# Block 2 of a two-block transformer kernel: modulation products queued behind the first norm, and attention heads taken in pairs on halves of the systolic array

## The chip, the cores and the metric

One core of one Trainium2 chip runs one program. The metric is the device time of one execution in microseconds, the median of the runs taken. The core has engines with a queue of instructions each: TensorE (PE; its weight loads are shown as PEld), VectorE (DVE), ScalarE (ACT), GpSimd (POOL) and SyncE (SP), which issues most transfers. Each engine runs its queue in the order that was fixed when the program was built; across engines they wait for each other by semaphores. Matrix products write into eight PSUM banks, which the kernel calls `g`, `u`, `l` (two each), `t` and `f`.

## The reference

256 tokens of width 1024 in float32 go through a first block (linear attention, block attention and a product-key mixture of experts) and then through a second block of two layers. The change lies in the second. Its first layer mixes with attention, its second with a convolution, and each has an MLP with a squared ReLU behind its mixer:

```python
mod = (c_act @ ada_w[l] + ada_b[l])[:, None, :]
sh1, sc1, g1, sh2, sc2, g2 = jnp.split(mod, N_MOD, axis=-1)
h = modulate(x, sh1, sc1)
...
x = layer_norm(DEEPNORM_ALPHA * x + g1 * y, ln_g[l, 0], ln_b[l, 0])
h = modulate(x, sh2, sc2)
x = layer_norm(DEEPNORM_ALPHA * x + g2 * sq_relu_mlp(h, mlp_w1[l], mlp_w2[l]), ln_g[l, 1], ln_b[l, 1])
```

The attention of the first layer has two groups. Group a is a differential attention of 4 heads: each head has two query and key halves of 64, two softmaxes over 512 keys (256 of a context, 256 of the tokens), and the second softmax times a factor is taken from the first ahead of the values, of width 128. Group b has 8 query heads of 64 that share 2 key and value heads. The outputs of both, side by side, go through `attn_w_out`. The modulation vectors `mod` are a product of one row, the activated conditioning vector, with a matrix of 1024 x 6144 for each layer.

## The kernel before

Products that need float32 accuracy are made of three products of halves: a value is cast to a shorter float `h` (ACT, L161, or DVE), the remainder `l = raw - h` is a difference on DVE (L165) or POOL (L167), and TensorE adds `h*h`, `l*h` and `h*l` (L219 to L221 with the tokens as columns, L251 with the tokens as rows). Weights stream from HBM into `raw` tiles, by SP's queue, and get these two parts.

A scheduler sets the order of each engine's queue when the program is built, from the order in which the code is written and from simulated times. Three things override it: `issue_after(x)` puts an instruction behind `x` in the order, `in_turn()` keeps a series of products in the order in which it is written, and `behind_all` adds a real wait.

The modulation is not done on TensorE: `ada_stream` brings the matrix of both layers in 96 pieces of 128 x 1024 (`araw`, 512 KB each), and `products` multiplies each by the row `crow` and sums it into a column of `modT` (L281, one DVE operation), to which a bias is added (L282). The stream is spread over the whole program: `more(n)` emits the next n pieces, and 16 of them fall in the first MLP of block 2, whose code follows the first norm.

Group a's softmaxes come first (`a_probs`, a call for each half of 128 queries). For each of its 4 heads it calls `probs` (L1224 to L1229) for rows 0 to 63 and then for rows 64 to 127 of the query and key tiles: three products of 64 rows by 512 columns into one `u` bank (L1228), then `softmax_parts`: a maximum (L497), its negation (L499), an exponential with a sum (L503), a reciprocal (L505). Their difference is transposed by TensorE (L1234) and copied out (L1220 on ACT, L1222 on DVE, in turn). Between these lie dense products (L251) of the projections. `a_rows` makes the values (L1254).

Group b's loop follows (L1321 to L1344): for each half of the queries, four pairs of neighbouring heads 2hp and 2hp + 1, which share one key and value head and so lie on the same 64 rows. Each head gets `probs`, a scaling (L1336), four transposes (L1234) and four value products (L1340), which write the half `i` of 64 partitions of one bank `po`. A trace has two rows for each float32 product of this kind. The first products of `awo`, the output projection, for group a's half of the rows (`mx1`) lie between the pairs; the pieces 2 and 3 of `awo` for group b's half (`mx2`) come behind.

The first norm is `ln_block` at L1363. For each half `tt` of the tokens it multiplies the projection by its gate (L1124), adds the residual (L1125), takes the statistics (L1130, L1132), the inverse root (L1099 to L1103) and scales (L1147). `normed_fm` then transposes (L1025), evicts with the modulation's scale and shift into `x0`, on DVE (L1029) for `tt = 0` and on ACT (L1031) for part of it, and makes the first products of the MLP with the first weight piece in full float32 (L1034). `normed_parts` splits `x0` into `b8h` and `b8l` (L1045, L1046) behind the last scaling; its last instruction is what `behind_fm[1]` names, and it releases POOL's two products and two sums for the residual (L1155, L1156). `ln_block` is called four times; the second and third (the MLP's norm of layer one and the conv's of layer two) follow the same path.

## Time and profile before

| what | us |
|---|---|
| median of 3 runs | 1659.31 |
| lowest and highest | 1656.79, 1660.22 |
| the profiled execution | 1664.88 |
| its span | 1663.1 |
| mean granted clock of TensorE | 0.991 |

The profiled execution is one of its own, 5.6 us above the median; the trace's times start at its span's start. Block 2's group a softmaxes lie at about 1043 to 1092, group b's loop at 1104 to 1167, the first norm at 1155 to 1190, the second at 1357 to 1380, the third at 1457 to 1480. A row of the timeline gives start, duration, engine, line, operation, output and inputs, and how many like it follow; products are pipelined, so the length of a group is read from its first start to the next group's start.

### The profile page before, as it was taken

Reading aid. Unit: us, or ns where it says so; the run is one execution under the profiler, and the core shown is the slowest. Engines: PE = TensorE matmul, PEld = TensorE weight load, DVE = VectorE, ACT = ScalarE, POOL = GpSimd, SP = SyncE. Lnnn points to the kernel's source line nnn. Section 1 sums busy time; section 2 is a strip of 40 time slices with the busy share of each in tenths; the row PEclk is TensorE's granted clock in tenths of the full one; section 3 lists DMA queues with packets and bytes.
Section 4 is the critical chain, followed back from the end, with each engine's and each line's share of the span. In section 5 each row is a group of like instructions: output and inputs, shape, how many; then the busy total and the mean of one; then the engine's idle time right before and its main releaser. Section 6 shows DMA issues by size and latency. Waiting matters only on the chain.

```text
span 1663.1 us, 27669 instructions
## 1 busy us (share of the span) xinstructions
PE 1590.0 (96%) x10543; PEld 1405.8 (85%) x10543; DVE 1301.2 (78%) x2587; ACT 832.3 (50%) x1346; POOL 309.0 (19%) x219
## 2 busy tenths in 40 slices
PE   8999999999999999999999989999799999989997
PEld 5878989999999897777777778777789989989996
DVE  5777999999999988989888765686896457575445
ACT  5644433677766654444444453554454435444442
POOL 3302000233333320000000023210511124051112
PEclk9999999999999999999999999999999999999999
DMA  7424435555554468888899872031686536445540
GB/s 292 156 73 153 140 117 183 185 171 171 159 163 150 152 208 287 305 305 318 294 337 324 277 267 76 17 137 76 227 315 217 187 117 240 166 169 211 181 175 26
DMA packets 70840, 321.17 MB, mean 193 GB/s; under 512 B 7841, under 2 KB 8114, under 8 KB 54962
## 3 DMA queue, kind: packets, MB, share of 16 engines
q1 hardware_dynamic: 67808, 309.61, 54.5%
q10 hardware_dynamic: 2898, 9.78, 1.7%
q8 instruction: 83, 1.36, 0.3%
q14 instruction: 51, 0.42, 0.1%
HBM read 318.31 MB, written 1.05 MB: 192 GB/s over the span
## 4 chain that ended last, share of the span: by engine, by line
PE 51%; DVE 22%; DMA 15%; issue 7%; ACT 4%; POOL 1%; SPq 0%; DVEq 0%; ACTq 0%; POOLq 0%
PE g L251 12%; DMA araw<-in_ada_dram 7%; PE u L251 6%; DVE lu L165 5%; DMA raw<-in_vt_dram 5%; PE l L220 3%; PE l L219 3%; PE l L221 3%; PE l L864 3%; PE l L862 3%; PE l L863 3%; DVE araw L281 2%; DVE obx L896 2%; DMA raw<-in_ut_dram 2%; PE g L220 1%
## 5 line engine op out<-in xcount | busy, mean ns | idle before, releaser
L161 ACT CAST hu<-raw 128x1024 fp32r<-128x1024 f32 x244 | 256.2, 1050 | 283.3 <-DMA raw<-in_vt_dram 141.7
L165 DVE TENSOR_TENSOR l<-raw,h 128x1024 fp32r<-128x1024 f32 (+1 forms) x216 | 277.9, 1320 | 128.8 <-ACT h L161 128.8
L161 ACT CAST h<-raw 128x1024 fp32r<-128x1024 f32 x226 | 225.5, 1051 | 223.8 <-PE l L220 62.8
L165 DVE TENSOR_TENSOR lu<-raw,hu 128x1024 fp32r<-128x1024 f32 (+1 forms) x244 | 274.3, 1128 | 45.8 <-ACT hu L161 42.5
L862 PE MATMUL l<-xh,hu 128*128 128x256 f32 x928 | 261.6, 282 | 3.5 <-ACT act L872 2.6
L864 PE MATMUL l<-xh,lu 128*128 128x256 f32 x928 | 259.6, 281 | 4.0 <-DVE lu L165 3.9
L863 PE MATMUL l<-xl,hu 128*128 128x256 f32 x928 | 258.6, 279 | 0.0
L864 PEld LDWEIGHTS l<-xh,lu 128*128 128x128 f32 x928 | 174.5, 189 | 6.2 <-DVE lu L165 6.0
L862 PEld LDWEIGHTS l<-xh,hu 128*128 128x128 f32 x928 | 175.2, 189 | 4.6 <-ACT act L872 3.2
L863 PEld LDWEIGHTS l<-xl,hu 128*128 128x128 f32 x928 | 175.4, 189 | 0.1
L167 POOL TENSOR_TENSOR lu<-raw,hu 128x256 fp32r<-128x256 f32 x92 | 106.6, 1160 | 341.2 <-ACT hu L161 292.6
L167 POOL TENSOR_TENSOR l<-raw,h 128x512 fp32r<-128x512 f32 (+1 forms) x32 | 61.2, 1936 | 571.9 <-ACT h L161 510.0
L281 DVE SCALAR_TENSOR_TENSOR araw<-araw,crow 128x1024 f32<-128x1024 f32 x96 | 121.8, 1270 | 25.5 <-DMA araw<-in_ada_dram 25.2
L219 PE MATMUL l<-b8h,h 128*128 128x256 f32 x480 | 134.8, 281 | 1.2 <-ACT rl L1367 1.2
L220 PE MATMUL l<-b8l,h 128*128 128x256 f32 x480 | 134.8, 281 | 0.0
L221 PE MATMUL l<-b8h,l 128*128 128x256 f32 x480 | 134.5, 280 | 0.0
L896 DVE SCALAR_TENSOR_TENSOR obx<-cst,slotT,gpair 128x256 f16<-128x256 f32 x256 | 131.6, 540 | 1.6 <-PE u L903 1.5
L1369 POOL TENSOR_TENSOR rq<-rl 128x512 f32<-128x512 f32 x32 | 54.4, 1702 | 236.1 <-ACT rl L1367 227.8
L957 PE MATMUL g<-lu,hw 128*128 128x512 f32 x256 | 83.2, 406 | 14.8 <-DVE lu L165 14.4
L219 PEld LDWEIGHTS l<-b8h,h 128*128 128x128 f32 x480 | 90.9, 190 | 1.5 <-ACT rl L1367 1.4
L221 PEld LDWEIGHTS l<-b8h,l 128*128 128x128 f32 x480 | 90.9, 190 | 0.0
L220 PEld LDWEIGHTS l<-b8l,h 128*128 128x128 f32 x480 | 90.2, 188 | 0.1
(555 smaller groups left out, 3707.7 us busy)
## 6 DMA issues: line engine op xcount, KB each, us to landing
raw<-in_ut_dram SPq DMA_DIRECT2D x128, 512.0 KB, 4.0
raw<-in_vt_dram SPq DMA_DIRECT2D x128, 512.0 KB, 5.3
raw<-in_mw_dram SPq DMA_DIRECT2D x64, 1024.0 KB, 5.0
araw<-in_ada_dram SPq DMA_DIRECT2D x80, 512.0 KB, 5.3
raw<-in_cwi_dram SPq DMA_DIRECT2D x12, 1024.0 KB, 5.0
raw<-in_w_ina_dram SPq DMA_DIRECT2D x8, 1024.0 KB, 8.0
raw<-in_wq_dram SPq DMA_DIRECT2D x8, 1024.0 KB, 4.8
raw<-in_awi_dram SPq DMA_DIRECT2D x8, 1024.0 KB, 7.2
```

Source lines behind the costliest of these rows:

```text
L161: S.copy(h[:, c:c + w], src[:, c:c + w])
L165: V.tensor_sub(l[:, c:m], src[:, c:m], h[:, c:m].bitcast(F32))
L167: G.tensor_sub(l[:, m:c + w], src[:, m:c + w], h[:, m:c + w].bitcast(F32))
L219: PE.matmul(o, hw, xh[:, k, :], start=k == 0, stop=False)
L220: PE.matmul(o, hw, xl[:, k, :], start=False, stop=False)
L221: PE.matmul(o, lw, xh[:, k, :], start=False, stop=k == KD - 1)
L251: PE.matmul(o[:, :cw], st, mv[:, c:c + cw], start=first and kk == 0 and i == 0, stop=last and kk == kp - 1 and i == 2)
L281: V.scalar_tensor_tensor(raw, raw, 1.0, crow, ALU.mult, ALU.mult, accum_out=d)
L862: PE.matmul(o, hv[:, k], xh[:, k], start=k == 0, stop=False)
L863: PE.matmul(o, hv[:, k], xl[:, k], start=False, stop=False)
L864: PE.matmul(o, lv[:, k], xh[:, k], start=False, stop=k == KD - 1)
L896: V.scalar_tensor_tensor(ob, C("iota")[:, None, :].to_broadcast([P, 2, P]), slotT[:, 0, t:t + 1], gpair[:, t, :, None].to_broadcast([P, 2, ...
```

## The change

It has four parts.

1. `behind_fm` is made ahead of the stream of modulation pieces, and each product L281 that is emitted once it is set is ordered behind `behind_fm[1]`, the last `b8l` of the norm. It is empty until the first norm, so the first products concerned are the 16 of the first MLP.
2. `to_fm` may scale: the queries of both groups are stored times -0.125. `probs` then takes a minimum of the negated scores as the exponential's bias and -1 as its scale. The 32 negations (L499) of these heads are gone.
3. `probs` makes the scores of both row halves, six products that alternate between rows 64 to 127 and 0 to 63, in written order, into two `u` banks. Group a uses it for the two halves of a head. Group b's loop pairs heads h and h + 4, which use different key heads and so different row halves; the 16 rows of their value products alternate between the column halves 64 to 127 and 0 to 63. `PB`, the table of banks, goes.
4. As the heads' outputs now stand in pairs h, h + 4, the rows of `awo` in pieces 2 and 3 are brought in that order: each `raw` tile by two transfers of 64 partitions, both tiles issued ahead of the product.

```diff
-    behind = []
+    behind, behind_fm = [], []
...
-            V.scalar_tensor_tensor(raw, raw, 1.0, crow, ALU.mult, ALU.mult, accum_out=d)
+            with tc.issue_after(behind_fm[1]) if behind_fm else ExitStack():
+                V.scalar_tensor_tensor(raw, raw, 1.0, crow, ALU.mult, ALU.mult, accum_out=d)
...
+                if scale:
+                    S.activation(dh, pv, AF.Identity, scale=scale)
+                    V.scalar_tensor_tensor(dst[1][:, b0:b0 + nb, c0:c0 + T], pv, scale, dh.bitcast(F32), ALU.mult,
+                                           ALU.subtract)
+                    continue
...
-    def probs(qT_, kT_, qb, kb, hs, qt, tag="u"):
-        ps = bank(tag)
+    def probs(qT_, kT_, qb, kb, qt):
+        pss = [bank("u"), bank("u")]
         q_ = slice(qt * P, (qt + 1) * P)
+        next_to = in_turn()
         for n, (i, j) in enumerate(((0, 0), (0, 1), (1, 0))):
-            PE.matmul(ps, qT_[i][hs, qb, q_], kT_[j][hs, kb], start=n == 0, stop=n == 2)
-        return softmax_parts(ps, 512, sm, 512)
+            for g in (1, 0):
+                hs = slice(g * 64, g * 64 + 64)
+                next_to(pss[g], qT_[i][hs, qb, q_], kT_[j][hs, kb], start=n == 0, stop=n == 2)
+        er = []
+        for ps in pss:
+            nm = sm.tile([P, 1], F32, tag="snm", name="snm")
+            V.tensor_reduce(nm, ps, AX.X, ALU.min)
+            e = sm.tile([P, 512], F32, tag="se", name="se", bufs=4)
+            s = sm.tile([P, 1], F32, tag="ssum", name="ssum")
+            S.activation(e, ps, AF.Exp, scale=-1.0, bias=nm, accum_out=s)
+            r = sm.tile([P, 1], F32, tag="srec", name="srec")
+            V.reciprocal(r, s)
...
-            e0, r0 = probs(aqT, akT, h, h, slice(0, 64), qt, PB[qt][2 * h])
-            e1, r1 = probs(aqT, akT, h, h, slice(64, 128), qt, PB[qt][2 * h + 1])
+            (e0, r0), (e1, r1) = probs(aqT, akT, h, h, qt)
...
-            for i in range(2):
-                h = 2 * hp + i
-                g = h // 4
-                e, r = probs(bqT, bkT, h % 4, 0, slice(g * 64, g * 64 + 64), qt)
+            pts = []
+            for e, r in probs(bqT, bkT, hb, 0, qt):
                 V.tensor_scalar(e, e, r, None, ALU.mult)
-                pt = transposed(e)
-                for kt in range(4):
-                    PE.matmul(po[i * 64:i * 64 + 64, :P], bv[:, kt, g * 64:g * 64 + 64], pt[:, kt * P:(kt + 1) * P],
-                              start=kt == 0, stop=kt == 3)
+                pts.append(transposed(e))
+            next_to = in_turn()
+            for kt in range(4):
+                for g in (1, 0):
+                    next_to(po[g * 64:g * 64 + 64, :P], bv[:, kt, g * 64:g * 64 + 64], pts[g][:, kt * P:(kt + 1) * P],
+                            start=kt == 0, stop=kt == 3)
...
-    gemm_tm(wp, hp2, rows_of("awo", 2, 4), 1024, *mx2, oacc, begun=True)
+    raws = []
+    for q in range(2):
+        raws.append(wp.tile([P, 2048], F32, tag="raw", name="raw"))
+        rv = raws[q].rearrange("p (k n) -> p k n", k=2)
+        for g in range(2):
+            queued(rv[g * 64:g * 64 + 64], a["awo"][2 + g].rearrange("(i p) (k n) -> k p i n", i=2, k=2)[q])
+    gemm_tm(wp, hp2, raws, 1024, *mx2, oacc, raw=True, begun=True)
```

In the changed kernel the products made through `in_turn()` are recorded under the helper's line, L182; L251 is L250 there, L1228's scores and L1340's values are both L182, L1234 is L1255.

TensorE's queue in group b's loop, first half of the queries. Before, the six scores of a pair (`u<-bkT..`), eight rows of transposes (`l<-cst,se`), then eight value products:

```order
L1228 MATMUL u<-bkTh,bqx 128x512
L1228 MATMUL u<-bkTl,bqx 128x512
L1228 MATMUL u<-bkTh,bqx 128x512 x2
L1228 MATMUL u<-bkTl,bqx 128x512
L1228 MATMUL u<-bkTh,bqx 128x512
L1234 MATMUL l<-cst,se 128x128 x8
L1340 MATMUL f<-pt,bv 64x128 x8
L1228 MATMUL u<-bkTh,bqx 128x512
L1228 MATMUL u<-bkTl,bqx 128x512
L1228 MATMUL u<-bkTh,bqx 128x512 x2
L1228 MATMUL u<-bkTl,bqx 128x512
L1228 MATMUL u<-bkTh,bqx 128x512
```

And in the changed kernel, about the same place:

```order
L182 MATMUL u<-bkTh,bqx 128x512 x2
L182 MATMUL u<-bkTl,bqx 128x512 x2
L182 MATMUL u<-bkTh,bqx 128x512 x2
L1255 MATMUL l<-cst,se 128x128 x8
L182 MATMUL u<-bkTh,bqx 128x512
L182 MATMUL t<-pt,bv 64x128 x8
L182 MATMUL u<-bkTh,bqx 128x512
L182 MATMUL u<-bkTl,bqx 128x512 x2
L182 MATMUL u<-bkTh,bqx 128x512 x2
L1255 MATMUL l<-cst,se 128x128 x8
```

The partners of a pair stand next to each other now; the next pair's first score product has moved ahead of this pair's values, away from its five others.

DVE's queue at the first norm, where `b8h` and `b8l` are the split parts of its output, `araw` the modulation pieces and `l<-raw,h` the MLP's weight differences. Before:

```order
L281 SCALAR_TENSOR_TENSOR araw,modT<-araw,crow 128x1024
L1102 TENSOR_SCALAR qt<-qy,qh 128x1
L282 TENSOR_TENSOR modT<-modT,col 128x1
L1103 TENSOR_SCALAR qy<-qt,qy 128x1
L1147 TENSOR_SCALAR xn<-xn,mv,qy 128x512 x2
L1045 CAST b8h<-x_12732 128x4x128 x2
L1046 TENSOR_TENSOR b8l<-x_12732,b8h 128x4x128 x2
L1045 CAST b8h<-x_12732 128x2x128
L281 SCALAR_TENSOR_TENSOR araw,modT<-araw,crow 128x1024
L1045 CAST b8h<-x_12732 128x2x128
L1046 TENSOR_TENSOR b8l<-x_12732,b8h 128x2x128
L1045 CAST b8h<-x_12732 128x2x128 x2
```

In the changed kernel nothing stands between the scaling and the casts, and the casts and differences stand alone up to these rows, from the last two of each on:

```order
L1050 CAST b8h<-x_12670 128x2x128
L1051 TENSOR_TENSOR b8l<-x_12670,b8h 128x2x128
L1050 CAST b8h<-x_12670 128x2x128
L1051 TENSOR_TENSOR b8l<-x_12670,b8h 128x2x128
L281 SCALAR_TENSOR_TENSOR araw,modT<-araw,crow 128x1024 x2
L164 TENSOR_TENSOR l<-raw,h 128x1024 x2
L282 TENSOR_TENSOR modT<-modT,col 128x1
L164 TENSOR_TENSOR l<-raw,h 128x1024
L282 TENSOR_TENSOR modT<-modT,col 128x1
L164 TENSOR_TENSOR l<-raw,h 128x1024
L281 SCALAR_TENSOR_TENSOR araw,modT<-araw,crow 128x1024
```

All modulation products of this stretch have moved behind the last `b8l`, two of them ahead of the first weight differences.

ACT's queue at the second norm, with the evictions of its output (`x`, L1031, in the changed kernel L1036) and the casts of the next weights (`h<-raw`). Before:

```order
L1099 ACTIVATE qs<-mv,epst 128x1
L1031 ACTIVATE x_14431<-l,mods 128x128 x3
L1031 ACTIVATE x_14431<-t,mods 128x128 x2
L1031 ACTIVATE x_14431<-l,mods 128x128
L1031 ACTIVATE x_14431<-f,mods 128x128 x2
L161 CAST h<-raw 128x1024 x4
L1031 ACTIVATE x_14431<-l,mods 128x128 x4
```

And in the changed kernel:

```order
L1104 ACTIVATE qs<-mv,epst 128x1
L1036 ACTIVATE x_14369<-l,mods 128x128 x7
L1036 ACTIVATE x_14369<-t,mods 128x128 x2
L1036 ACTIVATE x_14369<-f,mods 128x128 x2
L160 CAST h<-raw 128x1024 x4
```

The four casts have moved behind the last evictions. The third norm has the same rows, before and after, with another number behind `x`.

## Rows read from the trace of the kernel before

**Rows 1.** The page's first part: busy time of each engine, its share of the span, and instructions.

```profile
PE 1590.0 (96%) x10543; PEld 1405.8 (85%) x10543; DVE 1301.2 (78%) x2587; ACT 832.3 (50%) x1346; POOL 309.0 (19%) x219
```

**Rows 2.** Busy time by stretch: start and end, length, then PE, PEld, DVE, ACT and POOL with their instructions, the mean granted clock of TensorE, the DMA share and GB/s. Group a's softmaxes, group b's loop, the first norm and what follows it.

```profile
1043.00:1090.00 47.00, 46.68 (x273) 36.97 (x272) 33.63 (x103) 26.49 (x58) 6.56 (x5) 1.00 0.23 90
1104.00:1167.00 63.00, 59.45 (x341) 44.85 (x340) 43.85 (x116) 27.39 (x63) 2.42 (x2) 0.97 0.23 84
1167.20:1209.00 41.80, 31.43 (x249) 30.32 (x247) 38.29 (x56) 19.58 (x31) 22.02 (x8) 0.92 0.68 239
```

**Rows 3.** PE's timeline in group a's part, one group of three score products and what follows it: start, duration, engine, line, operation, output and inputs, rows, columns.

```profile
1070.64 0.50 PE L1228 MATMUL u<-akTh,aqTh 64*128 64x512 f32 x1
...
1071.53 0.39 PE L251 MATMUL g<-h,cxl 128*128 128x256 f32 x1
```

**Rows 4.** PE's timeline in group b's loop, one cycle of a pair.

```profile
1127.28 0.49 PE L1228 MATMUL u<-bkTh,bqx 64*128 64x512 f32 x1
...
1128.87 1.10 PE L1234 MATMUL l<-cst,se 128*128 128x128 f32 x8
1130.21 1.58 PE L1340 MATMUL f<-pt,bv 128*64 128x128 f32 x16 [0.24 <-ACT pt L1220]
1131.72 0.50 PE L1228 MATMUL u<-bkTh,bqx 64*128 64x512 f32 x1
```

**Rows 5.** The same timeline in the second half of the queries, the value products of one head and what follows.

```profile
1143.52 1.09 PE L1340 MATMUL l<-pt,bv 128*64 128x128 f32 x8
1144.54 0.66 PE L1234 MATMUL l<-cst,se 128*128 128x128 f32 x4
```

**Rows 6.** PE's timeline in block 1, products through `in_turn()` (L183) on the two row halves, then on the two column halves, then on quarters.

```profile
97.34 0.71 PE L183 MATMUL u<-mkT,mqT 64*128 64x128 f32 x6
97.98 0.71 PE L523 MATMUL u<-cst,cst 128*128 128x128 f32 x4
...
112.86 0.66 PE L183 MATMUL l<-gv,at 128*64 128x128 f32 x8
113.45 0.45 PE L183 MATMUL l<-st,eb 64*64 64x128 f32 x8
```

**Rows 7.** The views of lines L1228 and L1340, what PE sat idle for ahead of them (us, times), and of L499, whose row gives least, median and most ns.

```profile
  ACT se L503: 8.2, 5
...
  ACT pt L1220: 4.2, 9
...
L499 DVE TENSOR_SCALAR snm<-sm x48: 134/144/155, 78.7 to 1150.2; 128x1 f32<-128x1 f32 x48
```

**Rows 8.** DVE's and ACT's timelines in group b's loop: both reductions of a pair, a copy of the transposes, an exponential and its read-out.

```profile
1119.35 1.28 DVE L497 TENSOR_REDUCE sm<-u 128x1 f32<-128x512 f32 x2
1120.55 0.68 DVE L1222 COPY pt<-l 128x512 f32<-128x512 f32 x1
...
1121.44 0.69 ACT L503 ACTIVATE se<-u,snm 128x512 f32<-128x512 f32 x1
1122.03 0.20 ACT L503 ACTIVATION_READ_ACCUMULATOR se<-u,snm 128x1 f32 x1
```

**Rows 9.** The chain of waits from the end of group b's loop through the first norm, in order of time: start, us, what.

```profile
1167.19 3.90 DMA araw<-in_ada_dram
1171.11 3.01 DVE araw L281 x2
1174.14 5.30 DMA araw<-in_ada_dram
1179.47 1.23 DVE araw L281 x2
...
1184.26 1.14 DVE araw L281 x2
...
1187.81 0.75 DVE b8l L1046 x2
1188.56 3.53 DVE l L165 x2
```

**Rows 10.** The timelines of DVE and POOL behind the first norm.

```profile
1196.37 2.06 DVE L281 SCALAR_TENSOR_TENSOR araw<-araw,crow 128x1024 f32<-128x1024 f32 x1
...
1198.36 3.40 DVE L165 TENSOR_TENSOR l<-raw,h 128x1024 fp32r<-128x1024 f32 x1
1201.69 3.41 DVE L281 SCALAR_TENSOR_TENSOR araw<-araw,crow 128x1024 f32<-128x1024 f32 x1
...
1188.64 6.66 POOL L1155 TENSOR_TENSOR xres<-xn,lrow 128x1024 f32<-128x1024 f32 x2 [15.62 <-DVE b8l L1046]
```

**Rows 11.** The chain of waits at the second norm and at the third.

```profile
1371.86 3.77 ACT h L161 x4
...
1376.04 4.22 PE g L1034 x32
...
1468.72 1.51 ACT x L1031 x4
1470.23 3.77 ACT h L161 x4
...
1474.41 5.78 PE g L1034 x32
```

More of the change, by code (lines that the diff above doesn't have):

```diff
@@ L35 @@
 NWARM = 9
-PB = "uuuuuuuu", "uuuuuuuu"
 EVV = 1, 0
@@ L427, in norm_rope, with to_fm @@
         return s4
-    def to_fm(src, nh, dst, c0=0, tag="u"):
+    def to_fm(src, nh, dst, c0=0, tag="u", scale=None):
         s3 = src.rearrange("p t h d -> p t (h d)")
@@ L1014, in pair @@
         return [xp2.tile([P, KD, T], F32R, tag="b8", name=n, bufs=2) for n in ("b8h", "b8l")]
-    behind_fm, hp3 = [], []
+    hp3 = []
     def normed_fm(src, tt, scale, shift, x0, w0, o0):
@@ L1212 @@
     aq = norm_rope(prj, 8, rcv, rsv, sw2, 16, V, pj, "ak", norm=False)
-    to_fm(aq, 8, aqT, 0, AQT)
+    to_fm(aq, 8, aqT, 0, AQT, -0.125)
     mx1 = [at.tile([P, 4, T], F32R, name="mx1" + c) for c in "hl"]
@@ L1314 @@
     bqT = bqx[:, 0], bqx[:, 1]
-    to_fm(bq, 8, bqT, 0, BQT)
+    to_fm(bq, 8, bqT, 0, BQT, -0.125)
     a_rows(1, pts)
@@ L1322 @@
     for qt in range(NT):
-        for hp in range(4):
-            j = qt * 4 + hp
+        for hb in range(4):
+            j = qt * 4 + hb
             for pc, tt, ns in MXO.get(j, ()):
```

7 lines of the change are left out of this document (5 added, 2 removed).

## The prediction

> **What bounds the kernel now.** The page first: PE is busy 96% of the span, DVE 78% [rows 1]. The span is mostly TensorE work, and a change gains in two ways only: fewer TensorE microseconds, or smaller holes between them. Then the table by stretches, for the places that the diff touches [rows 2]. In block 2's attention PE is nearly full: 46.68 of 47.0 us in group a's part, 59.45 of 63.0 us in group b's. At the first norm it is not: 31.43 of 41.8 us, 10.4 us of holes, with a granted clock of 0.92 on average. PE's timelines show what attention's work is made of [rows 3 to 6], the chain of waits shows what the norms' holes wait for [rows 9, 11]. The issue orders come last, for what moves without being named in the diff.
>
> **Part 1: score and value products in pairs.** A head's scores are three products of 64 rows by 512 columns. One group alone takes 0.89 us, 1070.64 to 1071.53 [rows 3]; two in sequence, on one row half and then on the same or the other, 1.59 us, 1127.28 to 1128.87 [rows 4]. Inside, a product follows the last after 0.23 us; the rest, some 0.2 us, is the step into 64-row work and out. Do products on different halves of the array run side by side? No row shows it for 512 columns on two row halves, so I bound it by block 1. There eight products on alternating column halves take 0.59 us, 112.86 to 113.45 [rows 6], 0.074 each, against 0.094 each for the sixteen value products of today (1.51 us, 1130.21 to 1131.72 [rows 4]). Eight on row and column quarters last 0.45 us as a group where those on column halves last 0.66. But six on the two row halves take 0.64 us, 97.34 to 97.98 [rows 6], 0.107 each: no gain by the mean. So the bounds for a pair of score groups are 0.99 us (three steps of 0.23, and in and out) and 1.59 us (no overlap). I take 0.99 to 1.05 where the six stand together, nearest to the column row, since the alternation is fixed in the order. The value products of a pair, 16 in eight steps: 0.97 us (8 x 0.109 and the step in), against 1.51 in the first half of the queries and 2 x 1.02 in the second, where each head's eight stand alone [rows 5].
>
> In group a's part the order cuts most pairs: one score product, some dense ones of 256 columns, then the other five. A cut pair steps in and out twice, about 1.4 us, against two neighbouring groups of 0.89 (1.69 with a shared step). In the second four pairs today's groups are cut themselves (0.99 each), and of the new pairs two are whole and two cut (1.2 on average). PE work: 4 x (1.69 - 1.41) + 4 x (1.98 - 1.2) = 4.2 us. PE is full there, so nearly all of it reaches the end; but the last two pairs stand back to back and meet the softmax. I take **3.0 us** (bounds 0 and 4.5).
>
> *A rule against this.* The step in and out is some 0.2 us [rows 3, 4]. The Trainium skill, "TensorEngine Tiling (Array Packing)", Tiling Modes, Key Properties, says that changing the tiling mode drains TensorE. The trace agrees as far as the step goes; by that rule a splintered order gives the overlap back, and were all sixteen pairs cut as the first are, the sum would be about 3 us smaller.
>
> In group b's part eight pairs save 8 x (1.59 - 0.99) = 4.8 us on scores, less five cuts at 0.2 = 3.8, and 4 x 0.54 + 4 x 1.07 = 6.4 us on values: 10.2 us of PE work. What is late next is the softmax: two reductions (1.28 us together), two exponentials of 0.69 with a read-out of 0.20 each, a scaling, a copy of 0.68 [rows 8]. With two score banks, the next pair's first product waits for this pair's last exponential: scores 0.9, reductions 1.3, the last exponential 0.9 and hand-overs, 3.3 to 3.8 us per pair. The cycle now is 4.44 us (1127.28 to 1131.72 [rows 4]). So pairs without dense products between them gain 0.7 to 1.1 us, those with dense products of `awo` beside them 1.2 to 1.6, their full saving less some wait. Waits for these results are small today: 8.2 us over both parts for exponentials, 4.2 for copies [rows 7]. I take **7.5 us** (bounds 3 and 11).
>
> The minimum in place of a negated maximum drops 32 operations of 0.144 us [rows 7], 4.6 us of DVE, 0.29 per pair; it lies in the loop just bounded and is counted there. `to_fm` has as many operations as before. The `awo` pieces come as four transfers of 512 KB for two of 1 MB, on the same queue at the same place, behind the same transfers and far ahead of their first reader. Zero for both, give or take 0.5 us; were that cover gone, one transfer's time would show.
>
> **Part 2: modulation products behind the first norm.** Attention's last product ends at 1167.2. Then the chain [rows 9] is not the norm's own: DVE takes an `ada` product of 3.01 us at 1171.11, waits 5.30 us for the next transfer to 1179.47, takes that product (1.23), and has two more (1.14, and one like it) among the casts. The last `b8l` ends at 1188.56. Foreign pieces: 3.01 + 5.30 + 1.23 + 2 x 1.14 = 11.8 us; less about 1.0 of the norm's statistics and square root that run inside them: 10.8 us gained, the last `b8l` at 1177.8. PE's 10.4 us of holes agree [rows 2].
>
> Paid back: the products still have to run. Two of them stand ahead of the first weight difference (L165), more between the next ones, and all of DVE's queue waits behind each. The same `b8l` releases POOL's products for `xres`, 6.66 us for two [rows 10], and beside POOL, DVE's operations with two inputs in SBUF take 2.06 to 3.41 us in place of 1.2. So two products cost 2.4 to 6.8 us before L165; TensorE has the second half's first products and the pieces whose differences are ready to cover some of it. I take 2.8 back, net **8.0 us** (bounds 0 and 10.8).
>
> *A rule against this too.* Beside POOL's 3.3 us operations DVE's take up to 3.41 us, alone 1.23 [rows 9, 10]. The Trainium skill, "SBUF — State Buffer", says that DVE and GpSimd take a shared port pair by an exclusive lock held for a whole instruction. The trace agrees. If every product behind the norm paid it, the net would be about 4 us in place of 8; this is rival 2.
>
> **Part 3: norms two and three, a side effect.** The order shows that these move too. Before, ACT does most of the second half's evictions (L1031), then four weight casts (L161, 3.77 us), then the last evictions; the first weight products (L1034) wait for those: casts at 1371.86, then 1376.04 for PE, and casts at 1470.23 in the third norm [rows 11]. After, all eight evictions come first, and the casts behind. The chain loses 3.77 us twice. Late next: the casts start some 1.5 us later (four evictions of 0.38 us each go first) and have the 32 products L1034 (4.22 and 5.78 us) as cover for the main product; L165 stands behind all casts of `x`, and meets POOL. I take 3.3 and 4.2 us (the 5.78 may become 4.2), less 1.5 for L165: **6.0 us** (bounds -1 and 8).
>
> **Sum.** 3.0 + 7.5 + 8.0 + 6.0 = 24.5 us. Profiled execution 1664.9 - 24.5 = 1640.4 us; it lay 5.6 us above the median of the runs, 1659.3, so against that 1634.8: **1635 us**.
>
> **Rivals.**
> 1. *Row halves don't overlap.* For: the 64-row products at 97.34. Against: those on quarters [rows 6]. Then scores gain nothing: a 0, b about 4 from values; 18 us in all, 1641.
> 2. *Products crowd DVE behind the first norm.* Five of them at up to 3.4 us meet POOL, and PE waits for L165: of the norm's 8 us 0 to 2 are left. For: [rows 10]. Against: PE's holes come before L165 today, not behind it. 17.5 us, 1642.
> 3. *Norms two and three give nothing*, since casts and L165 are late instead: 18.5 us, 1641.
> 4. *Slower.* A pair holds both score banks. If PE then went through each pair in sequence (0.9 + 1.3 + 1.8 + 0.5 + 0.55 + 0.7 + 1.0 = 6.7 us for 4.44), sixteen pairs would lose 36 us where the norms gain 14: 1681 at worst; a milder form, or the clock's 1.2 GHz level through the holes, 1663 to 1670. It decides from about 5.4 us per pair (14 / 16 above today's). Against: the next pair's scores are ordered ahead of this one's transposes and values.
> 5. *The change doesn't do what it says:* the order cuts every pair. 3 us less, 1638; in the range anyway.
>
> **How the numbers follow.** Forecast with rival 5 0.67; rivals 1, 2 and 3 0.09, 0.11 and 0.07, all still faster; rival 4 0.04; two of rivals 1 to 3 with small attention gains, no change, 0.02. Half the width of the four pairs of bounds is 2.3, 4, 5.4 and 4.5 us, 8.4 as independent terms; with 2 us between runs about 9. The range 1623 to 1649 holds that and each of rivals 1 to 3 alone. About 0.2%, 3.3 us, is what a measurement of this kernel tells from no change: faster by more 0.94, within 0.02, slower 0.04.
>
> **What would show it.** Right: a pair's six score products in about 1 us and its values in 0.97; group b's part some 55 us long for 63; at the first norm no `ada` product between attention's end and the last `b8l`, and that 11 us nearer; norms two and three without L161 in the chain between evictions. Rival 2: L281 rows above 3 us behind the norm, and holes of PE there. Wrong: holes of PE of more than 15 us in attention, or the main product behind the first norm less than 5 us nearer to attention's end.

## The result, and the profile after

The changed kernel takes 1645.08 us, the median of 4 runs (1641.12 to 1645.86), against 1659.76 us before: 14.7 us less. The ratio is 0.9896, 95% interval 0.9863 to 0.9929. In a second series of runs it is 1645.79 against 1661.46 us, 0.9892 (0.9867 to 0.9918); between them the two intervals allow a gain of 12 to 23 us. Its first profiled execution took 1644.43 us, span 1642.6 us.

What a reader compares is not the two spans but stages that begin and end with the same instruction. I take six starts on TensorE and the end: group a's first score product, the ninth product of `awo` with group a's rows (which ends group a's part), the first transposes of the first norm, the first product on the first MLP's `mh`, the first on the convolution's `cvh`, and the first on the second MLP's `mh`. Lengths between them, in us:

| profile | first score at | group a | group b | first norm | first MLP, second norm, conv | its output, third norm | second MLP to the end | from the first score |
|---|---|---|---|---|---|---|---|---|
| before | 1043.1 | 61.0 | 61.0 | 42.2 | 232.7 | 56.4 | 166.7 | 620.0 |
| before, second profile | 1043.0 | 60.9 | 61.2 | 41.9 | 236.3 | 56.1 | 166.7 | 623.2 |
| changed | 1041.5 | 62.9 | 55.5 | 33.6 | 229.7 | 51.3 | 168.1 | 601.0 |
| changed, second profile | 1045.8 | 63.0 | 55.5 | 33.5 | 231.6 | 51.8 | 167.5 | 602.9 |

From group a's first score on, the changed kernel is 17 to 22 us shorter, and most stages repeat within 0.5 us. Two things scatter more. Ahead of the first score, where the change does nothing, its start moves by 4 us between the two profiles of the changed kernel; and the stage with the first MLP moves by 3.6 us between those of before. Group a got longer by 1.9 us; group b, the norms and what follows them got shorter. The bounds don't part equal work everywhere: of the 48 products of `awo` with group b's rows, group b's stage holds 42 before and 46 after. At one each 0.23 us, 0.9 us of work moved from the first norm's stage into group b's.

The page's first part of the changed kernel, which answers to [rows 1]: the change took 12 us of TensorE's work, and DVE was busy 11 us longer. The page's groups say where: the 216 weight differences `l<-raw,h` take 289.6 us for 277.9, the modulation products hardly less than before (120.1 for 121.8).

```profile
PE 1578.2 (96%) x10543; PEld 1396.3 (85%) x10543; DVE 1312.4 (80%) x2555; ACT 833.5 (51%) x1346; POOL 302.9 (18%) x219
```

The table by stretches of both kernels, with the stages' own ends as bounds, so other rows than [rows 2]; columns as there. Before:

```profile
1043.10:1104.10 61.00, 59.25 (x356) 48.38 (x356) 47.05 (x148) 37.70 (x78) 11.04 (x7) 0.97 0.18 71
1104.10:1165.10 61.00, 57.45 (x330) 43.17 (x328) 42.74 (x113) 26.57 (x60) 2.32 (x2) 0.97 0.23 86
1165.10:1207.20 42.10, 32.34 (x255) 31.44 (x255) 37.70 (x55) 19.00 (x32) 22.02 (x8) 0.92 0.66 230
```

After:

```profile
1041.50:1104.40 62.90, 59.17 (x349) 47.73 (x348) 46.80 (x132) 37.60 (x77) 12.29 (x9) 0.95 0.21 69
1104.40:1159.90 55.50, 49.98 (x342) 35.68 (x341) 41.90 (x98) 27.14 (x62) 1.12 (x1) 1.00 0.29 94
1159.90:1193.40 33.50, 29.02 (x243) 27.88 (x242) 32.16 (x43) 19.27 (x32) 22.09 (x8) 1.00 0.62 220
```

In group a PE is busy as long as before, and idle 2 us longer. In group b it has 7.5 us less to do and is idle 5.5 us, not 3.6. At the first norm its holes shrink from 9.8 to 4.5 us. The granted clock moved too: from 0.97 to 0.95 in group a, from 0.97 to 1.00 in group b and from 0.92 to 1.00 at the first norm, so a part of the busy times is the clock's.

TensorE's timeline in group b after, one cycle and a half; it answers to [rows 4]:

```profile
1117.56 0.50 PE L182 MATMUL u<-bkTh,bqx 64*128 64x512 f32 x1
1117.56 0.73 PE L182 MATMUL u<-bkTl,bqx 64*128 64x512 f32 x2
1117.90 0.63 PE L182 MATMUL u<-bkTh,bqx 64*128 64x512 f32 x2
1118.46 0.65 PE L1255 MATMUL l<-cst,se 128*128 128x128 f32 x4
...
1124.11 0.50 PE L182 MATMUL u<-bkTh,bqx 64*128 64x512 f32 x1 [0.97 <-ACT se L1245]
1124.54 1.09 PE L182 MATMUL t<-pt,bv 128*64 128x128 f32 x16
1125.57 0.50 PE L182 MATMUL u<-bkTh,bqx 64*128 64x512 f32 x1
```

The partners start together (1117.56 twice): 512 columns on two row halves do overlap. Sixteen value products take 1.03 us, 1124.54 to 1125.57, for 1.51. But the next pair's first score product waits 0.97 us for an exponential (1124.11), in a place where TensorE waited 0.24 us for a copy before.

Around the first norm, DVE's timeline after, which answers to [rows 9, 10]:

```profile
1172.38 0.43 DVE L1051 TENSOR_TENSOR b8l<-x,b8h 128x256 fp32r<-128x256 f32 x1
1172.72 1.22 DVE L281 SCALAR_TENSOR_TENSOR araw<-araw,crow 128x1024 f32<-128x1024 f32 x1
...
1173.87 3.40 DVE L281 SCALAR_TENSOR_TENSOR araw<-araw,crow 128x1024 f32<-128x1024 f32 x1
...
1177.20 6.74 DVE L164 TENSOR_TENSOR l<-raw,h 128x1024 fp32r<-128x1024 f32 x2
```

and PE's and POOL's, the two holes that are left and what runs beside the differences:

```profile
1180.67 0.39 PE L220 MATMUL l<-b8h,l 128*128 128x256 f32 x1 [1.22 <-DVE l L164]
1183.99 0.39 PE L220 MATMUL l<-b8h,l 128*128 128x256 f32 x1 [1.67 <-DVE l L164]
...
1172.89 6.65 POOL L1160 TENSOR_TENSOR xres<-xn,lrow 128x1024 f32<-128x1024 f32 x2 [6.06 <-DVE b8l L1051]
```

The last `b8l` ends 12.9 us after the norm's first transposes (1159.9 to 1172.8), where it took 23.5 (1165.1 to 1188.6). Then the first weight differences take 3.4 us each beside POOL, and TensorE waits 2.9 us for them.

The chain of waits at the third norm after, which answers to [rows 11]:

```profile
1450.23 3.17 PE g L1039 x26
...
1454.69 1.86 ACT x L1036 x5
1456.56 3.30 ACT h L160 x4
```

The evictions end ahead of the casts, as the order said.

### The profile page after: what moved, and what is told of

Its sections match the earlier page's. It is cut to its first block, busy times and chain, and to the rows that moved or that the text cites. A ratio compares the mean times of both kernels' runs of the same rounds, so it can differ in the third digit from the quotient of the medians.

```text
span 1642.6 us, 27643 instructions
## 1 busy us (share of the span) xinstructions
PE 1578.2 (96%) x10543; PEld 1396.3 (85%) x10543; DVE 1312.4 (80%) x2555; ACT 833.5 (51%) x1346; POOL 302.9 (18%) x219
## 4 chain that ended last, share of the span: by engine, by line
PE 58%; DVE 17%; DMA 13%; issue 7%; ACT 4%; POOL 1%; SPq 0%; DVEq 0%; ACTq 0%; POOLq 0%
PE g L250 12%; PE u L250 7%; DMA raw<-in_vt_dram 5%; DMA araw<-in_ada_dram 5%; PE l L869 4%; PE l L867 4%; PE l L868 4%; DVE lu L164 4%; PE l L218 3%; PE l L219 3%; PE l L220 3%; DVE l L164 2%; DVE obx L901 2%; DMA raw<-in_ut_dram 2%; DVE araw L281 2%
## 5 line engine op out<-in xcount | busy, mean ns | idle before, releaser
L164 DVE TENSOR_TENSOR l<-raw,h 128x1024 fp32r<-128x1024 f32 (+1 forms) x216 | 289.6, 1374 | 114.7 <-ACT h L160 114.6
L160 ACT CAST h<-raw 128x1024 fp32r<-128x1024 f32 x226 | 226.3, 1053 | 227.3 <-PE l L219 56.1
L166 POOL TENSOR_TENSOR l<-raw,h 128x512 fp32r<-128x512 f32 (+1 forms) x32 | 61.2, 1936 | 561.4 <-ACT h L160 504.8
L281 DVE SCALAR_TENSOR_TENSOR araw<-araw,crow 128x1024 f32<-128x1024 f32 x96 | 120.1, 1253 | 22.4 <-DMA araw<-in_ada_dram 22.4
```

The lines of the kernel that those rows point to most:

```text
L160: S.copy(h[:, c:c + w], src[:, c:c + w])
L164: V.tensor_sub(l[:, c:m], src[:, c:m], h[:, c:m].bitcast(F32))
L166: G.tensor_sub(l[:, m:c + w], src[:, m:c + w], h[:, m:c + w].bitcast(F32))
L281: V.scalar_tensor_tensor(raw, raw, 1.0, crow, ALU.mult, ALU.mult, accum_out=d)
```

## The experiments

Twelve runs followed, each with its own profile: ten new kernels, and the two from above once more. Medians, ratios to the kernel before (same chip, same series; worked out from all runs, so not the quotient of the medians) with 95% intervals, and the stages as above:

| run | median us | ratio | group a | group b | first norm | MLP, 2nd norm, conv | 3rd norm | 2nd MLP |
|---|---|---|---|---|---|---|---|---|
| after_again (changed) | 1645.79 | 0.9892 (0.9867-0.9918) | 63.0 | 55.5 | 33.5 | 231.6 | 51.8 | 167.5 |
| e1_behind_only | 1648.96 | 0.9922 (0.9902-0.9942) | 60.8 | 62.5 | 34.4 | 229.6 | 51.3 | 168.2 |
| e2_pairs_only | 1653.30 | 0.9944 (0.9922-0.9967) | 63.1 | 56.5 | 39.7 | 232.8 | 51.9 | 167.6 |
| e3_a_alone | 1651.16 | 0.9936 (0.9913-0.9960) | 68.4 | 59.5 | 35.5 | 229.4 | 51.3 | 168.1 |
| e4_xres_late | 1637.01 | 0.9841 (0.9810-0.9872) | 62.8 | 55.2 | 30.1 | 228.8 | 51.3 | 166.6 |
| e5_a_by_head | 1647.28 | 0.9899 (0.9873-0.9926) | 67.7 | 53.3 | 33.5 | 229.5 | 51.3 | 168.1 |
| e6_b_scores_apart | 1638.84 | 0.9867 (0.9843-0.9890) | 62.8 | 52.6 | 33.6 | 229.7 | 51.3 | 168.1 |
| e7_both | 1643.46 | 0.9874 (0.9845-0.9903) | 68.8 | 54.8 | 29.7 | 229.3 | 51.3 | 166.6 |
| e8_evict_in_turn | 1659.49 | 0.9980 (0.9966-0.9994) | 62.2 | 60.9 | 41.9 | 232.5 | 51.3 | 168.2 |
| e9_a_before | 1641.90 | 0.9880 (0.9857-0.9902) | 60.9 | 56.3 | 33.9 | 229.4 | 51.9 | 167.5 |
| e10_a_before_late | 1640.20 | 0.9852 (0.9827-0.9877) | 62.1 | 56.3 | 31.7 | 229.3 | 51.3 | 166.6 |

The twelfth, before_again, was a single execution of 1668.0 us (before in that series: 1663.56). The profiled execution of a kernel often lies above its median (1650.5 for 1645.8, 1655.4 for 1649.0), so stages are compared with stages and medians with medians.

**The kernels as they are.**

> The changed kernel once more, for a tighter interval and a second profile. My reading of the two profiles is 20.4 us between them, while the medians differ by 14.7 us: I expect 13 to 18 us below the kernel before (ratio 0.989 to 0.992), since the first profile of before lay some 5 us above that kernel's own median. Rival: the first four runs happened to lie high, then about 20 us (0.988).

> The kernel before once more, profiled, to see where two profiles of one kernel differ. Theory: the scatter of some 5 us lies in block 1 ahead of group a's scores, and from there on the stages repeat within 1 us. Rival: the norm's waits for modulation transfers vary by several us, so that the first profile's 10 us hole was not typical.

The first theory held, with 15.7 us between the medians. The second held in part. Five of the six stages of before repeat within 0.3 us, the first norm's among them (41.9 us), so its holes were typical and the rival is out. But group a's first score starts at the same time in both, and the 3.6 us between them lie in the stage with the first MLP: 1.5 in the MLP itself and 1.7 in the convolution, the same 1.7 us that set the changed kernel's 231.6 apart from 229.7. Set against the medians, the 20 us between the first two profiles were partly chance.

**The two parts alone.** e1 adds part 1 of the change, the modulation products ordered behind the norm, to the kernel before:

```diff
-            V.scalar_tensor_tensor(raw, raw, 1.0, crow, ALU.mult, ALU.mult, accum_out=d)
+            with tc.issue_after(behind_fm[1]) if behind_fm else ExitStack():
+                V.scalar_tensor_tensor(raw, raw, 1.0, crow, ALU.mult, ALU.mult, accum_out=d)
```

> The kernel before with part 1 alone: modulation products ordered behind the norm's last b8l. The order shows the second and third norms' evictions ahead of the weight casts here as well. Theory (stages add): attention as before; first norm 7 us shorter, second and third 3 to 3.6 us each: about 13 us less than before, 1646 to 1649. Rival (attention's pairs were needed to get the modulation transfers out of the way, so part 1 alone is worth little): less than 6 us.

e2 takes it away from the changed kernel:

```diff
-            with tc.issue_after(behind_fm[1]) if behind_fm else ExitStack():
-                V.scalar_tensor_tensor(raw, raw, 1.0, crow, ALU.mult, ALU.mult, accum_out=d)
+            V.scalar_tensor_tensor(raw, raw, 1.0, crow, ALU.mult, ALU.mult, accum_out=d)
```

> The changed kernel without the ordering of the modulation products: pairs, scale, awo rows alone. The order of the second and third norms is the changed one here too. Theory: attention 6 us shorter, first norm as before (products among its casts), norms two and three 6 us shorter together: 10 to 13 us less than before, 1647 to 1650. Rival (norms two and three gain from the products' order): 6 us less, 1654.

e1: 12.5 us below before, about the theory's 13. The first norm is 7.8 us shorter without any pair, so the rival is out. (Group b took 1.5 us longer there: its waits are those of before, but its products take 58.9 us for 57.5, at a granted clock of 0.95 for 0.97.) e2: 8.2 us below, less than the theory's 10 to 13. Group b is 4.5 us shorter; the first norm keeps 39.7 us, and the first MLP has a hole of 2.78 us where TensorE waits 0.62 us in the kernel before, 0.87 in e1 and 1.00 in the changed kernel:

```profile
1207.67 1.22 PE L250 MATMUL g<-h,ml 128*128 128x512 f32 x2 [2.78 <-DVE ml L1399]
```

So part 1 is worth some 9 us beside the pairs, 6 at the norm and 3 by keeping this hole shut. Against the kernel before it gains nothing in the MLP itself (155.8 us in e1 from its first product to its last, 155.6 before); e1's 3.1 us in that stage are the second norm's. The third norm's 4 to 5 us come with either part.

**Norms two and three.** e8 is the kernel before with the second half's evictions in written order:

```diff
-        g = FMG[tt]
+        g, ev_ = FMG[tt], []
...
-                    a_ = S.activation(o, p_, AF.Identity, scale=scale[:, c], bias=shift[:, c])
+                    with tc.issue_after(ev_[0]) if tt and ev_ else ExitStack():
+                        a_ = S.activation(o, p_, AF.Identity, scale=scale[:, c], bias=shift[:, c])
+                    ev_[:] = [a_.ins]
```

> The kernel before with one edit: the evictions of the second half of the tokens are ordered as written, so that at norms two and three all of them stand ahead of the weight casts. The order changes there and nowhere else. Theory (the side effect is a gain of its own, whatever else changes): the stage with the second norm 1 to 3 us shorter, the stage with the third norm 3.6 us, everything ahead as before: 5 to 7 us below the kernel before, ratio 0.996. Rival (those gains need the earlier weight pieces of the changed kernel): no change, 1.000.

3.4 us below before (0.998, an interval that excludes 1), for 5 to 7 expected. The third norm's stage falls from 56.4 to 51.3 us and 1.5 us are given back in the second MLP, as in the changed kernel: the order is the cause there. It is more than the casts, though. In the kernel before, TensorE waits there 2.27 us for an eviction that stands behind them, and 1.86 us for the first half's scaling (L1147), which DVE takes behind the second half's statistics. Both waits are gone in e8, with 0.68 us for a copy in their place.

The second norm's stage is shorter by 0.2 us only. In this profile the convolution had its 1.7 us of chance, and from the first MLP's last product to the 144th of the convolution it was 2.0 us shorter (33.5 to 31.5), where the changed kernel has 3.4 (30.1). TensorE's waits show the rest. In the kernel before there are two:

```profile
1366.05 1.89 PE L1025 MATMUL l<-cst,xn 128*128 128x128 f32 x8 [1.95 <-DVE xn L1147]
...
1376.04 4.22 PE L1034 MATMUL g<-x,raw 128*128 128x128 f32 x32 [1.38 <-ACT x L1031]
```

e8 lost the second of them and kept the first:

```profile
1365.93 1.59 PE L1025 MATMUL l<-cst,xn 128*128 128x128 f32 x8 [1.96 <-DVE xn L1149]
```

The changed kernel has neither, and a shorter one in their place:

```profile
1351.41 1.16 PE L1085 MATMUL f<-cst,modT 128*128 128x128 f32 x8 [0.68 <-ACT gb L1086]
```

e1 and e2 have the whole gain (30.1 and 29.9 us), so it comes with either part, by the orders that the scheduler then finds on ACT and on DVE.

**What part 1 pays back.** e4 moves POOL's products and sums for the residual from behind the last `b8l` to behind the last evictions of the next product:

```diff
-            for tt in range(NT):
-
-                behind_all(G.tensor_mul(xres[:, tt], xn[:, tt], lrow[:, 0]), last)
-                G.tensor_add(xres[:, tt], xres[:, tt], lrow[:, 1])
+            def residual(i):
+                for tt in range(NT):
+                    behind_all(G.tensor_mul(xres[:, tt], xn[:, tt], lrow[:, 0]), i)
+                    G.tensor_add(xres[:, tt], xres[:, tt], lrow[:, 1])
...
+                if i == 3 and todo:
+                    todo.pop()(v.ins)
```

> The changed kernel with POOL's residual products and sums of the first three norms moved behind the last evictions of the next product, so that they no longer run beside the weight differences right behind the norm. Theory (what part 1 paid back behind the first norm is POOL contention): the differences there take 1.2 us instead of 3.4, TensorE's two holes of 1.2 and 1.7 us go, and the second and third norms gain a little: 3 to 5 us below the changed kernel, ratio to the kernel before 0.986 to 0.988. Rival (the same POOL operations meet other differences later, and TensorE waits there): no change, 0.989, or slower.

The theory held, with more than the 3 to 5 us expected: 1637.0 us, ratio 0.9841, the lowest median of all, though the intervals of e6 and e10 overlap with its own. From the first score on it is 594.9 us long, 6.1 less than the changed kernel. DVE behind the first norm now:

```profile
1176.04 1.22 DVE L281 SCALAR_TENSOR_TENSOR araw<-araw,crow 128x1024 f32<-128x1024 f32 x1
...
1177.18 2.36 DVE L164 TENSOR_TENSOR l<-raw,h 128x1024 fp32r<-128x1024 f32 x2
```

The second product takes 1.22 us for 3.40, two differences 2.36 for 6.74, and PE has no hole between the last `b8l` and the first product on `mh`. The stage is 3.5 us shorter than in the changed kernel, and the 1.4 us that the second MLP gave back behind the third norm are gone (166.6). POOL's operations, now in the MLP, cost nothing that the stages show.

**Group a.** Three kernels treat its scores in other ways. e3 writes the halves one after the other, e5 writes the pair's six products half by half (and keeps the alternation in group b), and e9 has all of group a as before, maximum and negation too, so that the order there is that of the kernel before.

The line that calls for them in e3, what e5 changes in `probs`, and e9's calls, with `probs_old` and `probs1` for one half each:

```diff
-            (e0, r0), (e1, r1) = probs(aqT, akT, h, h, qt)
+            e0, r0 = probs1(aqT, akT, h, h, slice(0, 64), qt)
+            e1, r1 = probs1(aqT, akT, h, h, slice(64, 128), qt)
```

```diff
+        order = [(n, ij, g) for n, ij in enumerate(((0, 0), (0, 1), (1, 0))) for g in (1, 0)]
+        if not turn:
+            order.sort(key=lambda o: -o[2])
+        for n, (i, j), g in order:
...
+            (next_to if turn else PE.matmul)(pss[g], qT_[i][hs, qb, q_], kT_[j][hs, kb], start=n == 0, stop=n == 2)
```

```diff
-    to_fm(aq, 8, aqT, 0, AQT, -0.125)
+    to_fm(aq, 8, aqT, 0, AQT)
...
-            (e0, r0), (e1, r1) = probs(aqT, akT, h, h, qt)
+            e0, r0 = probs_old(aqT, akT, h, h, slice(0, 64), qt)
+            e1, r1 = probs_old(aqT, akT, h, h, slice(64, 128), qt)
```

> The changed kernel, but group a's score halves written one after the other as before, each with its own bank (minimum and scale as in the changed kernel). Theory (the old order already put the first four heads' halves side by side, and the written alternation only cuts them, so that pairing is worth nothing in group a): within 1.5 us of the changed kernel, rather faster, and group a's part ends no later. Rival (pairing in group a is worth the 3 us of the forecast, but a stall hides it): 2 to 3 us slower than the changed kernel.

> The changed kernel, but group a's pairs are written head half by head half, three products each, without the fixed alternation; group b keeps it. The order then has group a's first four pairs in six uncut products, and group b's in six for seven of eight. Theory (products on the two row halves overlap when they stand together in the queue, in whatever order; the cuts are what group a lost): group a's part some 2 us shorter, 61 us from its first score to the first product of awo, group b 1 to 2 us shorter than in the changed kernel: 2 to 4 us in all. Rival (overlap needs alternation in the queue): group a's first four pairs take 1.6 us each instead of 0.9, and the kernel is no faster than the changed one.

> The changed kernel with group a's scores and softmax as in the kernel before (maximum and negation, queries not scaled, halves written one after the other); group b, awo and the modulation products as changed. The order of TensorE in group a is then that of the kernel before, with its first four heads in uncut groups of six. Theory (group a loses 1.9 us by the change): group a's part 61 us, group b's 55.5 us, the rest as in the changed kernel: 2 us below the changed kernel, ratio 0.988. Rival (what group a loses is made up in group b, whose first scores wait for the same engines): no change against the changed kernel, 0.989.

Both theories were wrong on the time: group a takes 68.4 us in e3 and 67.7 in e5, longer than in either kernel. e3 didn't give the old order back: the softmax has one operation less than in the kernel before, and the scheduler set the two halves apart in seven of eight cases. e5's order did have the first four pairs whole, and they did overlap, though they are written half by half; the rows below are three pairs of starts, as they are with alternation:

```profile
1050.82 0.51 PE L1240 MATMUL u<-akTh,aqTh 64*128 64x512 f32 x2
1051.16 0.40 PE L1240 MATMUL u<-akTl,aqTh 64*128 64x512 f32 x2
1051.40 0.39 PE L1240 MATMUL u<-akTh,aqTl 64*128 64x512 f32 x2
```

What it loses is the end of group a's part, where the dense products have run out and TensorE waits for single softmaxes at a granted clock of 0.57:

```profile
1090.00:1106.00 16.00, 13.49 (x60) 11.17 (x61) 13.34 (x49) 10.35 (x19) 4.29 (x3) 0.57 0.08 17
```

e9 is the clean test: group a 60.9 us, and the kernel is 3.9 us below the changed one by medians of different series, a ratio of 0.988 against 0.9892, whose intervals overlap. The stage shows 2 us; group b gives 0.8 of them back. The clock has a part in it. With the order of before TensorE idles 1.75 us in group a in all six profiles, and the stage takes 60.8 to 61.0 us at a clock of 0.97 (both of before, e1, e9) but 62.2 and 62.1 at 0.95 (e8, e10). This is e8's:

```profile
1042.00:1104.20 62.20, 60.45 (x356) 49.37 (x356) 47.26 (x148) 37.60 (x78) 11.07 (x8) 0.95 0.18 69
```

The changed order idles 3.7 us and takes 62.8 to 63.1, at 0.95 each time. So what the change costs there is some 0.8 us at one clock and 2 us with the clock's fall.

**Both and best.** e7 joins e4 and e5, e10 joins e4 and e9.

> Both of the edits together, the residual products moved back and group a written by halves. Theory: the gains add, 5 to 8 us below the changed kernel, ratio to the kernel before 0.984 to 0.987. Rival (they share a wait, or the shift brings another order in the norms): no more than the better of the two.

> Group a as in the kernel before and, besides, POOL's residual products moved back: the best version that the runs point to. Theory (the stages add): 2 us below the run with the residual products alone, ratio 0.983. Rival: no better than that run, 0.984.

Neither is shown to beat e4. e7 carries e5's longer group a (68.8 us) and e4's shorter norm (29.7). In e10 the two gains don't add: group b takes 56.3 us and the first norm 31.7, the latter with holes as short as in e4 (1.6 us) but at a clock of 0.95 for 1.00.

**Group b.** e6 keeps the value products' alternation and writes the scores head by head, each head with its own bank.

```diff
-            for e, r in probs(bqT, bkT, hb, 0, qt):
+            for e, r in [probs1(bqT, bkT, hb, 0, slice(g * 64, g * 64 + 64), qt) for g in (0, 1)]:
```

> The changed kernel with group b's scores written head by head, three products each with its own bank, heads h and h + 4 still in turn; the value products keep their alternation. Most groups of three are cut from their partners by transposes in the order. Theory (of group b's 5.5 us about 3 are the values' and 2.5 the scores'): group b's part 57.5 to 58.5 us, 2 to 3 us slower than the changed kernel. Rival (the loop through the softmax sets the cycle, and a head alone gets through it sooner): group b as in the changed kernel or shorter.

The rival's forecast came true. Group b takes 52.6 us, 2.9 less than in the changed kernel, and the kernel 1638.84 us (0.9867, whose interval overlaps with the changed kernel's). The table of TensorE's waits in group b, engine, line, who for, us in total, times and the longest, the changed kernel first:

```profile
PE u L182 <- ACT se L1245: 3.8, 5, 1.3
PE f L182 <- ACT pt L1225: 0.7, 1, 0.7
```

and e6:

```profile
PE u L1233 <- ACT se L1238: 0.8, 1, 0.8
PE l L182 <- ACT pt L1225: 0.2, 1, 0.2
```

The stretch of e6 shows PE busy 51.05 of 52.5 us:

```profile
1101.10:1153.60 52.50, 51.05 (x340) 36.77 (x340) 40.64 (x99) 27.33 (x62) 1.20 (x1) 1.00 0.31 100
```

TensorE has 1.1 us more to do and 3.0 us less to wait for exponentials. So most of what group b gained is there without paired scores. The values' column halves are the likely cause (sixteen products in 1.03 us for 1.51), but no run has them alone.

Are the pairs what costs the 2.9 us? e5 speaks against it. Its group b has pairs too, and there the scheduler left seven of the eight with their six products together, where five are cut in the changed kernel. It takes 53.3 us, although all 48 products of `awo` lie in it (46 in e6), and waits less for exponentials than the changed kernel's 3.8 us; the stretch first, then the wait:

```profile
1111.00:1164.40 53.40, 49.95 (x344) 36.00 (x343) 39.67 (x98) 27.08 (x63) 0.00 (x0) 1.00 0.26 86
```

```profile
PE u L182 <- ACT se L1247: 2.4, 4, 1.4
```

From its fifth pair on no score product waits at all. In the changed kernel the product that waits at 1124.11 is a first one, cut from its pair. It needs one bank: it starts when the first of the two exponentials is over, and the second is still running. Nor could the values behind it have started much sooner, since the second copy of the transposes ends at 1124.04:

```profile
1123.28 0.69 ACT L1245 ACTIVATE se<-u,snm 128x512 f32<-128x512 f32 x1
...
1123.95 0.69 ACT L1245 ACTIVATE se<-u,snm 128x512 f32<-128x512 f32 x1
...
1123.36 0.68 DVE L1227 COPY pt<-l 128x512 f32<-128x512 f32 x1
```

The transposes of both heads came together just before (eight, from 1122.05), and TensorE had nothing else in its queue to do. In e5's loop the two heads' transposes stand apart, with six scores or sixteen values of other pairs between them.

So the 2.9 us are the price of pairs in the order that the scheduler gave them here; that pairing as such, or holding two banks at once, costs them is not shown. e5 is no clean test either, as its loop starts behind a longer group a. e4 and e6 were not joined; that would be the next version to try.

## Why the prediction was right, and where it was wrong

The time forecast, 1635 us in 1623 to 1649, holds the measured 1645; the forecast gain of 24.5 us was some 10 us too large against the medians, and 2 to 7 us too large by the stages, which show 17.1 to 22.2 us between the two profiles of each kernel. That the sum came as near as it did owes something to luck: group a's term had the wrong sign, group b's was helped by a rise of the clock that I hadn't counted, and that of norms two and three came out right although only one of its two waits was named. Term by term:

- **Group a, 3.0 us forecast, 1.9 us lost.** This step failed. It said that no row shows 512 columns on two row halves, and charged today's pairs 1.69 us. The trace of before has such rows, which I had not read, and I took the price of a pair from a lone group of the second half [rows 3] and from group b, whose two heads lie on the same rows [rows 4]:

```profile
1050.71 0.51 PE L1228 MATMUL u<-akTh,aqTh 64*128 64x512 f32 x2
1051.05 0.40 PE L1228 MATMUL u<-akTl,aqTh 64*128 64x512 f32 x2
1051.29 0.40 PE L1228 MATMUL u<-akTh,aqTl 64*128 64x512 f32 x2
```

  The first four heads' halves ran side by side already, as three close pairs, though the queue had them half by half. The change cut these pairs in two:

```profile
1049.68 0.50 PE L182 MATMUL u<-akTh,aqTh 64*128 64x512 f32 x1
...
1050.77 0.49 PE L182 MATMUL u<-akTh,aqTh 64*128 64x512 f32 x1
1050.77 0.72 PE L182 MATMUL u<-akTl,aqTh 64*128 64x512 f32 x2
```

  TensorE was busy as long as before (59.25 and 59.17 us), at a lower clock; against e8, whose clock there is the same 0.95, its work fell by 1.3 us (from 60.45), where I had counted 4.2. And it waits 2.0 us longer, most of it between the last two pairs, which stand back to back:

```profile
1089.33 0.49 PE L182 MATMUL u<-akTh,aqTh 64*128 64x512 f32 x1 [2.19 <-ACT se L1245]
```

  The lower bound of 0 that I gave had no room for this loss, although the stall was named in the same paragraph.
- **Group b, 7.5 us forecast, 5.5 measured.** The work was oversized and the waits were left out. I had counted 10.2 us less work. It fell by 7.5 us, and some 1.6 of these are the clock's: e2, with the pairs at the 0.97 of before, is busy 51.55 us for 57.45, 5.9 less, or 6.8 with the 0.9 us of `awo`'s products that moved in.

```profile
1107.60:1164.10 56.50, 51.55 (x342) 36.90 (x341) 41.90 (x98) 27.13 (x62) 1.03 (x1) 0.97 0.29 93
```

  The waits grew by 1.9 us. I had counted the loop through the softmax (3.3 to 3.8 us for a pair) and found it shorter than the cycle, and for a cut pair I charged 0.2 us, the step alone. But TensorE waits where its queue holds nothing else between a pair's transposes and the end of its softmax; in the orders of e5 and e6 fewer of these waits are left (2.4 and 0.8 us for exponentials, for 3.8). Rival 4 feared that TensorE would go through each pair in sequence; that happened in places, at a small part of the price of its worst case.
- **First norm, 8.0 us forecast, 8.6 measured.** The last `b8l` came 10.6 us nearer to the norm's first transposes (forecast 10.8), and 2.0 us were paid back (forecast 2.8). Of the 8.6 us, 0.9 are products of `awo` that moved into group b's stage. The payment is POOL's contention, as e4 shows, which gets 3.5 us back there. The Trainium skill, "SBUF — State Buffer", Who interferes with whom, says that a DVE instruction with two inputs in SBUF and a GpSimd instruction that reads SBUF contend for a shared port pair, which whichever issues first holds for the whole instruction; the trace agrees, with 3.40 us for a product beside POOL's 3.3 and 1.22 with POOL out of the way. In rival 2 the same contention took the whole gain; TensorE's holes behind the norm came to 2.9 us.
- **Norms two and three, 6.0 us forecast, 6.7 measured** in the first profile: 3.0 with the second norm, 5.1 with the third, 1.4 given back in the second MLP. The size was right, the mechanism half of it. I had taken the four casts' 3.77 us out of the chain twice, but what TensorE waited for an eviction behind them was 1.38 us at the second norm and 2.27 at the third. The rest came from the waits for the first half's scaling, 1.95 and 1.86 us, which the prediction didn't name, less 0.68 for the copy. e8 shows both for the third norm; for the second it shows the evictions' part, 2.0 us, and e1 and e2 the whole.
- **The sum against the median.** I took the profiled execution's 5.6 us above the median as an offset that carries over. The changed kernel's own offset was 0.65 below its median in the first profile and 4.7 above in the second. That is no term of the change; the stages from group a's first score on avoid it.
- The small operations and the four transfers for `awo` show no wait of their own in the profile.

## What to carry to other kernels

Before pricing a new overlap, look for it in the trace of before under the same line: products on different halves of the array may already start together when they only stand next to each other in the queue. When heads are taken in pairs, read in the queue's order what TensorE has to do while a pair's softmax runs: in the changed kernel both heads' transposes came together and it stood idle, in e5 they stood apart, and from the fifth pair on no score product waited. Compare stages at one clock, and count what lies in them, before a busy time is read as work. And when work is queued behind a critical result, look at what else the same result releases: here moving POOL's residual work away took another 6.1 us off the stages, where the whole change had taken 17 to 22.

## What was not expected of the hardware

Products on the two row halves need no alternation in the queue. In the kernel before the order of group a's first pair is

```
L1228 MATMUL u<-akTh,aqTh 128x512
L1228 MATMUL u<-akTl,aqTh 128x512
L1228 MATMUL u<-akTh,aqTl 128x512
L1228 MATMUL u<-akTh,aqTh 128x512
L1228 MATMUL u<-akTl,aqTh 128x512
L1228 MATMUL u<-akTh,aqTl 128x512
```

and the second pair's starts, with the same order, come in three couples (1050.71, 1051.05, 1051.29), each within 0.01 us; the six take 0.90 us, to 1051.61, where six on one row half take 1.59 [rows 4]. So TensorE began the other half's first product ahead of two that stood before it: the order of the queue is not the order of the starts here. For value products on column halves, eight and eight in the queue, it didn't reach as far: sixteen took 1.51 us [rows 4] and 1.03 in alternation. In rows 4 the second head's input may have come late, its copy ending at 1130.64; but sixteen others, begun at 1137.09 when both copies had been over for 2 us, took 1.51 us as well. And two short waits at the end of group a came with the lower of the two clock levels: 0.66 on average from 1090 to 1100 us in the changed kernel, 0.83 before, 0.57 over 16 us in e5.
